# End of mixer 0 in a hybrid streaming encoder step: copies on ScalarE, paired products and splits, scales one step from the root

## The chip, the core and the metric

The kernel runs on one core of a Trainium2 chip. The metric is device time in microseconds of one launch. Three runs of the kernel before gave 1126.33, 1127.34 and 1127.87 us (median 1127.34). The engines are named as in the profile: PE (TensorE matmul), PEld (its weight loads), DVE (VectorE), ACT (ScalarE), POOL (GpSimd) and SP (the queue that issues the weight transfers). Each works through its own instructions in order; between engines there are only semaphores.

## The reference

One step of a two-layer encoder for 256 frames of a new stream and 8 running streams of 16 frames: 384 columns in all. Layer 0 has two mixers from one input projection:

```python
xa, ga, qb, kb, vb, gb, zr = jnp.split(u @ w_in, cuts, axis=-1)
ha, new_h = rg_lru(xa, lru_h0, ...)          # linear recurrence over time
ya = ha * jax.nn.gelu(ga)
o, new_S = gla(heads(qb) * DK_B ** -0.5, heads(kb), heads(vb), heads(log_g), gla_S0)
o = rms_norm(o, g_norm)                      # per head, over its 256 columns
yb = o * jax.nn.silu(gb)
y = jnp.concatenate([ya, yb], axis=-1) @ w_out
```

Then come an RMS norm with residual, a SwiGLU block, and layer 1 (latent attention and another SwiGLU). The change lies where `ya` and `o` are finished and `y` begins.

## The kernel before

**Numbers in two halves.** Every float32 product is made of three matmuls of rounded operands: high with high, high with low, low with high (L287, L288, L289 in `mm3`). An operand `x` is split by a Copy on ACT into its high part and a subtraction on DVE into its low part (`split`, L315 and L316).

**Weights.** `Stream` brings blocks of eight 128x128 tiles. SP transfers a block into one of three raw buffers (L98), ACT copies the high half (`whi`, L110), DVE subtracts for the low half (`wlo`, L126). When PE begins block n, the split of block n + 2 is issued: its `whi` at once, its `wlo` once half of block n's tiles have been taken. A raw buffer is free for its next transfer after the `wlo`. One projection of eight tiles is one block, 24 matmuls; `proj` issues it and then calls `tick`.

**Side work.** `tick` takes each generator in the list `sides` one step further, to its next `yield`. Thus the recurrence (`lru`) and the matrix state (`states`) are issued a piece at a time between the projections of the main line. What is issued at one place enters the queues of its engines there, behind all that was issued earlier: that alone sets the order on each engine.

**The main line here.** After the projections `gb` come eight projections `ga` (here ga0 to ga7). `lru` ends with products, scans (L800) and its state `hl` during ga0 and ga1. Behind ga1 `drain` runs `tick` until `lru` is done. Each `ga` is multiplied by its row factor on DVE (L978) into a tile that the trace calls `sq`; after each second one the pair is finished: Gelu on ACT (L996), product with `hl` on DVE (L998), split into `yah` and `yal` (L315, L316). Then the output projection `out_ab` starts, four output tiles at a time, over 16 input tiles: eight `yah`/`yal`, then eight `ybh`/`ybl`. `yb` is called one input tile ahead; its first seven calls are a `tick` each, the first of them loading the ACT table for Ln and Exp and marking "gelu" as done.

**`states`.** The new stream is worked in two chunks j = 0 and 1 of 128 frames; j = 2 stands for the running streams. For each j, `intra` (L826), and for chunk 1 also L915, put two heads' output each into a bank of PSUM; `grow_new` (L856) makes the state's growth, which ACT copies to `S1` (L906; tile `S` in the trace). `take(j, hp, bank)` copies a bank to `on[j]` (L829) and squares each head on ACT with a running sum (L831). Chunk 0 is issued in the `drain` behind ga1, chunk 1's matmuls behind ga3, its `take` behind ga4. `on[0]` and `on[1]` use slots 13 and 14, where input states S0 lay that L883 reads. In the first `tick` of `out_ab`, Ln and Exp (L929, L930) turn the sums into factors; `scale(j)` multiplies `on[j]` head by head on DVE (L835); `otrans(j)` transposes it on PE (L842) and ACT copies the result to `oT` (L843), from which L1075 to L1078 make `ybh` and `ybl`.

Of the kernel before, what the change touches and what calls it, by code (L numbers as in the profile page):

```python
# [10 lines left out]
AF = mybir.ActivationFunctionType  # L11
# [165 lines left out]
def emit(ctx, tc, A, O):  # L177
    nc = tc.nc
    v_, s_, g_, pe = nc.vector, nc.scalar, nc.gpsimd, nc.tensor
# [13 lines left out]
    def slot(k, shape, dt=F32, name="sl"):  # L193
        return sp.tile(shape, dt, name=nm(name), tag=f"s{k}", bufs=1)
# [6 lines left out]
    def mm_hold():  # L201
        return pr_.tile("mm", 6, [P, 512], hold=True)

    def sd(shape=(P, T)):
        return pr_.tile("sd", 2, shape)
# [4 lines left out]
    def sqt():  # L210
        return tr.tile("sq", 2, [P, T])

    def acct():
        return tr.tile("acc", 1, [P, T])
# [4 lines left out]
    def small(shape, name, bufs=4):  # L219
        return tr.tile(name, bufs, shape)  # L220

    def f(ap):
        return ap.bitcast(F32)
# [51 lines left out]
    def tick():  # L275
        for g in list(sides):
            try:
                next(g)
            except StopIteration:
                sides.remove(g)  # L280

    def drain(g):
        while g in sides:
            tick()
# [29 lines left out]
    def split(hi, lo, src):  # L314
        s_.activation(hi, src, AF.Copy)  # L315
        v_.tensor_sub(lo, src, f(hi))  # L316
# [37 lines left out]
    def proj(mat, mt, xk=None, kts=KD, side=True):  # L354
        xk = xk or uk
        ps = mm()
        for kt in range(kts):
            mm3(ps, S.take(mat, kt, mt), xk(kt), kt == 0, kt == kts - 1)
        if side:
            tick()  # L360
        return ps
# [23 lines left out]
    def quads(tiles):  # L385
        return lambda i: tiles[i // 4][:, i % 4, :]
# [425 lines left out]
    def states():  # L812
        while "chunks" not in done:
            yield
        kdT, qe = late["kdT"], late["qe"]
        sqs = small([P, 3, H_B], "osq", 1)
        on = {}

        def vh(j, h):
            return vt[h // 2][:, j, (h % 2) * 256:(h % 2) * 256 + 256]  # L820

        def half(bank, h):
            return bank[:, (h % 2) * 256:(h % 2) * 256 + 256]

        def intra(j, bank, h, stop):
            pe.matmul(half(bank, h), at[:, j, h, :], vh(j, h), start=True, stop=stop)  # L826

        def take(j, hp, bank):
            v_.tensor_copy(on[j][:, 2 * hp:2 * hp + 2, :], bank.rearrange("p (h v) -> p h v", h=2))  # L829
            for h in (2 * hp, 2 * hp + 1):  # L830
                s_.activation(acct()[:, 0:256], half(bank, h), AF.Square, accum_out=sqs[:, j, h:h + 1])  # L831

        def scale(j):
            for h in range(H_B):
                v_.tensor_scalar(on[j][:, h, :], on[j][:, h, :], sqs[:, j, h:h + 1], None, op0=OP.mult)  # L835

        def otrans(j):
            for hf in range(2):
                ps = sd([P, 4, P])
                for i in range(4):  # L840
                    fb = hf * 4 + i
                    pe.transpose(ps[:, i, :], on[j][:, fb // 2, (fb % 2) * P:(fb % 2) * P + P], ident)  # L842
                s_.activation(oT[hf][:, :, j * P:(j + 1) * P], ps, AF.Copy)  # L843

        def grow(product):

            res = []
            for hp in range(2):
                ps = sd([P, 2, 256])
                for k in (2 * hp, 2 * hp + 1):  # L850
                    product(ps[:, k % 2, :], k)
                res.append(ps)
            return res

        def grow_new(j):
            return grow(lambda ps, k: pe.matmul(ps, kdT[:, j, k, :], vh(j, k), start=True, stop=True))  # L856


        s0t = {}

        def s0load(i):
            s0t[i] = slot((13, 14, 3)[i % 3], [P, 4, 256], name="S0")
            g_.dma_start(s0t[i], A["S0"][i])

        s0load(0)
        s0load(1)
        on[2] = slot(6, [P, H_B, 256], name="on")
        for _ in range(2):
            yield
        while vt[1] is None:  # L870
            yield
        s0load(2)
        for i in range(2 * H_B):
            h, b0 = i // 2, 4 * (i % 2)
            if i % 4 == 0:
                bank, free = mm_hold()
            if b0 == 0:
                intra(2, bank, h, False)
            st = s0t.pop(i)
            for k in range(4):  # L880
                b = b0 + k
                o0 = 32 * (b // 2)
                pe.matmul(half(bank, h)[o0:o0 + 32], qe[:, 1 + b % 2, h, o0:o0 + 32], st[:, k, :],  # L883
                          start=False, stop=(b % 2 == 1))
            if i + 3 < 2 * H_B:
                s0load(i + 3)
            yield
            if i % 4 == 3:
                take(2, h // 2, bank)
                free()  # L890
        done.add("sample")

        while hl[1] is None:
            yield
        oT[0] = slot(16, [P, 4, T], name="oT")
        oT[1] = slot(4, [P, 4, T], name="oT")
        S1 = slot(0, [P, H_B, 256], name="S1")
        on[0] = slot(13, [P, H_B, 256], name="on")
        on[1] = slot(14, [P, H_B, 256], name="on")
        banks = [mm_hold() for _ in range(2)]  # L900
        for h in range(H_B):
            intra(0, banks[h // 2][0], h, True)
        gs = grow_new(0)
        yield
        for hp in range(2):
            s_.activation(S1[:, 2 * hp:2 * hp + 2, :], gs[hp], AF.Copy)  # L906
        for hp in range(2):
            take(0, hp, banks[hp][0])
            banks[hp][1]()
        yield  # L910
        yield
        banks = [mm_hold() for _ in range(2)]
        for h in range(H_B):
            intra(1, banks[h // 2][0], h, False)
            pe.matmul(half(banks[h // 2][0], h), qe[:, 0, h, :], S1[:, h, :], start=False, stop=True)  # L915
        yield
        gs = grow_new(1)
        for hp in range(2):
            take(1, hp, banks[hp][0])
            banks[hp][1]()  # L920
        yield
        for h in range(H_B):
            v_.scalar_tensor_tensor(S1[:, h, :], S1[:, h, :], ebl[:, h, 1:2], gs[h // 2][:, h % 2, :],
                                    op0=OP.mult, op1=OP.add)
        yield
        g_.dma_start(O["pS"], S1)
        while "gelu" not in done:
            yield
        s_.activation(sqs, sqs, AF.Ln, scale=1.0 / 256, bias=epsc)  # L929
        s_.activation(sqs, sqs, AF.Exp, scale=-0.5)  # L930
        yield
        for j in range(5):
            yield
            if j < 3:
                scale(j)
            if j >= 2:
                otrans(j - 2)

    side_lru, side_states = lru(), states()
    sides += [side_states, side_lru]  # L940
    for hf in range(2):
# [33 lines left out]
    for i in range(8):  # L975
        ps = proj("ga", i)
        z = sqt()
        v_.tensor_mul(z, ps, r0)  # L978
        if i % 2 == 0:
            z0 = z  # L980
            if i == 0:
                assert "sqrt" in done
                for t in sg:
                    s_.activation(t, t, AF.Silu)
            continue
        if i == 1:
            drain(side_lru)
            yah = [slot(k, [P, 4, T], F32R, name="yah") for k in (10, 15)]
            yal = [slot(5, [P, 4, T], F32R, name="yal")]
            yah_at, yal_at, hl_at = quads(yah), quads(yal), quads(hl)  # L990
        if i == 5:
            while "sample" not in done:
                tick()
            yal.append(slot(3, [P, 4, T], F32R, name="yal"))
        for z in (z0, z):
            s_.activation(z, z, AF.Gelu_apprx_tanh)  # L996
        for k, z in ((i - 1, z0), (i, z)):
            v_.tensor_mul(z, z, hl_at(k))  # L998
            split(yah_at(k), yal_at(k), z)


    carry = slot(12, [P, 3, 512], name="carry")
# [647 lines left out]
    for hq in range(2):  # L1650
        ps = mm(512)
        for i in range(8):
            h = 8 * hq + i
# [172 lines left out]
```

## Time and profile before

| what | value |
|---|---|
| median of three runs | 1127.34 us (1126.33 to 1127.87) |
| profiled execution, its own time | 1128.62 us |
| its span, first to last instruction | 1126.8 us |
| PE busy | 1098.3 us, 97% |
| DVE busy | 667.4 us, 59% |
| ACT busy | 541.5 us, 48% |
| POOL busy | 160.5 us, 14% |
| mean granted TensorE clock | 0.992 of full |

Busy time is that in which an engine has an instruction at work. Matmuls are pipelined, so a row's duration is longer than the step from one to the next. A granted clock of 1.00 is 2.4 GHz, 0.50 is 1.2 GHz; a value between is a mean over both. All times in rows are microseconds from the span's start.

### The profile page before, as it was taken

Reading aid. Unit: us, or ns where it says so; the run is one execution under the profiler, and the core shown is the slowest. Engines: PE = TensorE matmul, PEld = TensorE weight load, DVE = VectorE, ACT = ScalarE, POOL = GpSimd, SP = SyncE. Lnnn points to the kernel's source line nnn. Section 1 sums busy time; section 2 is a strip of 40 time slices with the busy share of each in tenths; the row PEclk is TensorE's granted clock in tenths of the full one; section 3 lists DMA queues with packets and bytes.
Section 4 is the critical chain, followed back from the end, with each engine's and each line's share of the span. In section 5 each row is a group of like instructions: output and inputs, shape, how many; then the busy total and the mean of one; then the engine's idle time right before and its main releaser. Section 6 shows DMA issues by size and latency. Waiting matters only on the chain. (4 is left out here: it accounts for less than half of the span.)

```text
span 1126.8 us, 16586 instructions
## 1 busy us (share of the span) xinstructions
PE 1098.3 (97%) x6463; PEld 1044.1 (93%) x6463; DVE 667.4 (59%) x1062; ACT 541.5 (48%) x927; POOL 160.5 (14%) x230
## 2 busy tenths in 40 slices
PE   9999999799999999999999999899999999999997
PEld 8989989699999999999999988699899999999886
DVE  5898774766276765554333777789347545554333
ACT  5642567554456333334334566677545443333232
POOL 3225110000230100000011211256122000000000
PEclk9999999899999999999999999999999999999999
DMA  8332552135434763334343351334324333443442
GB/s 265 100 95 93 187 169 88 65 127 178 128 95 156 255 224 127 117 130 130 117 129 101 113 168 61 121 126 147 113 94 132 131 122 122 131 127 119 128 131 75
DMA packets 43375, 147.50 MB, mean 131 GB/s; under 512 B 4928, under 2 KB 7616, under 8 KB 43296
## 3 DMA queue, kind: packets, MB, share of 16 engines
q1 hardware_dynamic: 39504, 132.73, 36.8%
q0 software_dynamic: 3792, 13.70, 3.6%
q8 instruction: 51, 0.84, 0.3%
q14 instruction: 28, 0.23, 0.1%
HBM read 139.53 MB, written 6.88 MB: 130 GB/s over the span
## 5 line engine op out<-in xcount | busy, mean ns | idle before, releaser
L126 DVE TENSOR_TENSOR wlo<-wraw,whi 128x1024 fp32r<-128x1024 f32 (+1 forms) x232 | 279.7, 1206 | 268.0 <-ACT whi L110 267.6
L287 PE MATMUL mm<-uhi,whi 128*128 128x384 f32 x1016 | 349.9, 344 | 9.6 <-ACT whi L110 6.2
L289 PE MATMUL mm<-ulo,whi 128*128 128x384 f32 x1016 | 344.8, 339 | 0.8 <-DVE ulo L312 0.8
L288 PE MATMUL mm<-uhi,wlo 128*128 128x384 f32 x1016 | 343.9, 338 | 0.9 <-DVE wlo L126 0.9
L110 ACT ACTIVATE whi<-wraw 128x1024 fp32r<-128x1024 f32 (+1 forms) x232 | 244.1, 1054 | 201.5 <-PE mm L289 134.5
L287 PEld LDWEIGHTS mm<-uhi,whi 128*128 128x128 f32 x1016 | 192.9, 190 | 13.7 <-ACT whi L110 6.6
L289 PEld LDWEIGHTS mm<-ulo,whi 128*128 128x128 f32 x1016 | 192.2, 189 | 2.2 <-DVE ulo L312 2.2
L288 PEld LDWEIGHTS mm<-uhi,wlo 128*128 128x128 f32 x1016 | 192.0, 189 | 1.8 <-DVE wlo L126 1.5
L337 POOL TENSOR_TENSOR acc<-acc,sq 128x384 f32<-128x384 f32 x43 | 53.0, 1232 | 346.6 <-ACT sq L336 346.1
L315 ACT ACTIVATE ah<-tmp 128x384 fp32r<-128x384 f32 x44 | 23.1, 525 | 80.0 <-DVE tmp L1183 80.0
L287 PE MATMUL mm<-ah,whi 128*128 128x384 f32 x176 | 59.8, 340 | 0.0
L1179 ACT ACTIVATE tmp<-tmp 128x384 f32<-128x384 f32 x44 | 22.9, 524 | 75.9 <-DVE tmp L1178 75.8
L289 PE MATMUL mm<-al,whi 128*128 128x384 f32 x176 | 59.1, 336 | 0.0
L288 PE MATMUL mm<-ah,wlo 128*128 128x384 f32 x176 | 59.1, 336 | 0.0
L1180 DVE TENSOR_TENSOR tmp<-mm,r 128x384 f32<-128x384 f32 x44 | 24.4, 556 | 44.4 <-PE mm L289 44.4
L297 PE MATMUL mm<-whi,ah 128*128 128x512 f32 x120 | 47.2, 393 | 0.0
L299 PE MATMUL mm<-whi,al 128*128 128x512 f32 x120 | 46.9, 391 | 0.0
L298 PE MATMUL mm<-wlo,ah 128*128 128x512 f32 x120 | 46.6, 388 | 0.0
L121 POOL TENSOR_TENSOR wlo<-wraw,whi 128x512 fp32r<-128x512 f32 x22 | 32.0, 1455 | 68.6 <-ACT whi L110 51.0
L316 DVE TENSOR_TENSOR al<-tmp,ah 128x384 fp32r<-128x384 f32 x44 | 24.6, 558 | 26.0 <-ACT ah L315 26.0
L287 PEld LDWEIGHTS mm<-ah,whi 128*128 128x128 f32 x176 | 33.1, 188 | 0.0
L288 PEld LDWEIGHTS mm<-ah,wlo 128*128 128x128 f32 x176 | 33.0, 188 | 0.0
(376 smaller groups left out, 1901.5 us busy)
## 6 DMA issues: line engine op xcount, KB each, us to landing
wraw<-wst SPq DMA_DIRECT2D x214, 512.0 KB, 3.6
S<-S POOLq DMA_DIRECT2D x16, 512.0 KB, 5.1
wraw<-cT SPq DMA_DIRECT2D x8, 528.0 KB, 3.7
o_sS<-S POOLq DMA_DIRECT2D x8, 512.0 KB, 4.2
wraw<-cN SPq DMA_DIRECT2D x8, 512.0 KB, 3.6
h<-x SPq DMA_DIRECT2D x2, 768.0 KB, 5.9
wuk<-wukT SPq DMA_DIRECT2D x2, 768.0 KB, 6.5
o_y<-hrow SPq DMA_DIRECT2D x6, 256.0 KB, 2.0
```

The source lines that it names most:

```text
L110: self.nc.scalar.activation(hi[:, s], raw[:, s], AF.Copy)
L121: self.nc.gpsimd.tensor_sub(*(x[:, n:] for x in a))
L126: self.nc.vector.tensor_sub(*a)
L287: pe.matmul(out, wl[0], xr[0], start=start, stop=False)
L288: pe.matmul(out, wl[1], xr[0], start=False, stop=False)
L289: pe.matmul(out, wl[0], xr[1], start=False, stop=stop)
L297: pe.matmul(ps[:, cs], xs[0][:, js], wh, start=start and i == 0, stop=False)
L298: pe.matmul(ps[:, cs], xs[0][:, js], wl, start=False, stop=False)
L299: pe.matmul(ps[:, cs], xs[1][:, js], wh, start=False, stop=stop and i + n == 4)
L316: v_.tensor_sub(lo, src, f(hi))
L337: g_.tensor_add(self.acc, self.acc, q)
L1180: v_.tensor_mul(w, pu, r)
```

## The change

Three edits. `take` copies `on[0]` and `on[1]` with ACT instead of DVE; the running streams' `on[2]` stays on DVE. At each second `ga` the two columns are finished step by step together (two products, two Copies, two subtractions) instead of one column after the other. After Ln and Exp one `yield` is gone and the loop has six steps instead of five: `scale(0)`, `scale(1)`, `scale(2)` are each issued one `tick` earlier, the three `otrans` in the same `tick` as before.

```diff
         def take(j, hp, bank):
-            v_.tensor_copy(on[j][:, 2 * hp:2 * hp + 2, :], bank.rearrange("p (h v) -> p h v", h=2))
+            on_hp, src = on[j][:, 2 * hp:2 * hp + 2, :], bank.rearrange("p (h v) -> p h v", h=2)
+            if j < 2:
+                s_.activation(on_hp, src, AF.Copy)
+            else:
+                v_.tensor_copy(on_hp, src)
             for h in (2 * hp, 2 * hp + 1):
                 s_.activation(acct()[:, 0:256], half(bank, h), AF.Square, accum_out=sqs[:, j, h:h + 1])
...
         s_.activation(sqs, sqs, AF.Ln, scale=1.0 / 256, bias=epsc)
         s_.activation(sqs, sqs, AF.Exp, scale=-0.5)
-        yield
-        for j in range(5):
+        for j in range(6):
             yield
             if j < 3:
                 scale(j)
-            if j >= 2:
-                otrans(j - 2)
+            else:
+                otrans(j - 3)
...
         for z in (z0, z):
             s_.activation(z, z, AF.Gelu_apprx_tanh)
-        for k, z in ((i - 1, z0), (i, z)):
+        pair = (i - 1, z0), (i, z)
+        for k, z in pair:
             v_.tensor_mul(z, z, hl_at(k))
-            split(yah_at(k), yal_at(k), z)
+        for k, z in pair:
+            s_.activation(yah_at(k), z, AF.Copy)
+        for k, z in pair:
+            v_.tensor_sub(yal_at(k), z, f(yah_at(k)))
```

## Rows read from the trace of the kernel before

**Rows 1.** Waits of PE, whole span: waiter <- releaser: us in total, times, longest.
```profile
PE mm L287 <- ACT whi L110: 6.2, 1, 6.2
...
PE sd L842 <- DVE on L835: 1.3, 1, 1.3
```
**Rows 2.** Timeline of PE: start, busy us, line, out<-in, count, [idle before <- releaser].
```profile
214.78 0.59 PE L915 MATMUL mm<-S,qe 128*128 128x256 f32 x2
221.53 0.69 PE L287 MATMUL mm<-uhi,whi 128*128 128x384 f32 x1 [6.16 <-ACT whi L110]
222.79 0.69 PE L288 MATMUL mm<-uhi,wlo 128*128 128x384 f32 x1 [0.57 <-DVE wlo L126]
...
229.49 1.89 PE L856 MATMUL sd<-v,kdT 128*128 128x256 f32 x8
...
231.39 0.34 PE L288 MATMUL mm<-uhi,wlo 128*128 128x384 f32 x1
...
235.25 0.34 PE L289 MATMUL mm<-ulo,whi 128*128 128x384 f32 x1
...
243.85 0.34 PE L287 MATMUL mm<-yah,whi 128*128 128x384 f32 x1
```
**Rows 3.** Windows, the wait: busy us (instructions) by engine, granted clock, DMA share, GB/s.
```profile
218.00:220.00 2.00, 0.00 (x0) 0.00 (x0) 1.39 (x3) 0.71 (x2) 0.00 (x0) 0.56 0.00 0
```
**Rows 4.** Timeline of ACT, from the state's copies to `whi` of ga4.
```profile
203.80 1.06 ACT L906 ACTIVATE S<-sd 128x512 f32<-128x512 f32 x2
213.96 0.38 ACT L831 ACTIVATE acc<-mm 128x256 f32<-128x256 f32 x1 [9.09 <-DVE on L829]
...
215.96 1.28 ACT L996 ACT_TABLE_LOAD   x1
217.25 0.94 ACT L996 ACTIVATE sq<-sq 128x384 f32<-128x384 f32 x2
...
220.01 0.52 ACT L315 ACTIVATE yah<-sq 128x384 fp32r<-128x384 f32 x1 [1.09 <-DVE sq L998]
220.44 1.99 ACT L110 ACTIVATE whi<-wraw 128x1024 fp32r<-128x1024 f32 x2
```
**Rows 5.** Timeline of DVE, from column 1's L978 to `wlo` of ga4.
```profile
212.79 0.53 DVE L978 TENSOR_TENSOR sq<-mm,r 128x384 f32<-128x384 f32 x1
213.24 1.28 DVE L829 COPY on<-mm 128x512 f32<-128x512 f32 x2
...
219.43 0.55 DVE L998 TENSOR_TENSOR sq<-sq,hl 128x384 f32<-128x384 f32 x1
...
221.51 1.22 DVE L126 TENSOR_TENSOR wlo<-wraw,whi 128x1024 fp32r<-128x1024 f32 x1 [0.39 <-ACT whi L110]
```
**Rows 6.** Readers of S0 (L883): ns min/median/max, first and last start us, form.
```profile
L883 PE MATMUL mm<-S,qe x64: 379/379/403, 134.1 to 182.3; 128*32 128x256 f32 x64
```
**Rows 7.** Windows: behind the wait for `on`, and around 730 us.
```profile
252.00:253.00 1.00, 1.00 (x9) 0.88 (x9) 1.00 (x5) 0.60 (x2) 0.00 (x0) 1.00 0.61 152
...
730.00:735.00 5.00, 2.42 (x14) 2.26 (x15) 2.88 (x9) 2.90 (x8) 1.27 (x5) 0.87 0.48 149
735.00:740.00 5.00, 5.00 (x35) 5.00 (x35) 4.30 (x13) 3.33 (x11) 2.97 (x2) 0.79 0.31 93
```
**Rows 8.** Timeline of PE around the first two transpose groups.
```profile
250.00 0.34 PE L289 MATMUL mm<-yal,whi 128*128 128x384 f32 x1
...
252.64 0.42 PE L287 MATMUL mm<-yah,whi 128*128 128x384 f32 x1
...
254.64 0.34 PE L289 MATMUL mm<-yal,whi 128*128 128x384 f32 x1
255.61 0.42 PE L287 MATMUL mm<-yah,whi 128*128 128x384 f32 x1
```
**Rows 9.** Timelines of ACT and DVE: the root's Exp, and eight scalings of `on`.
```profile
248.91 0.21 ACT L930 ACTIVATE osq<-osq 128x12 f32<-128x12 f32 x1
...
251.25 2.18 DVE L835 TENSOR_SCALAR on<-on,osq 128x256 f32<-128x256 f32 x8
```

## The prediction

> **What bounds the kernel now.** The page's first part comes first: PE is busy 97% of the span, DVE 59%, ACT 48%, so only time in which PE waits, or runs at its lower clock, can be won. Next the waits of PE, longest first [rows 1]: the longest of the whole span, 6.2 us, is a matmul waiting for a `whi` tile (the high half of a weight block, written on ACT); one of 1.3 us waits for DVE's scaling of `on`. Both lie in the part that the change edits.
>
> The timeline of PE shows the first one [rows 2]. PE ends the matmuls of stream chunk 1 (L915, two of them, 214.78 + 0.59 = 215.37), and projection ga4 starts only at 221.53. Its second matmul waits again, for `wlo`, until 222.79. The granted clock makes it dearer [rows 3]: its mean of 0.56 over 218 to 220 says that it fell from 2.4 to 1.2 GHz about 218.2, after 2.9 us without a matmul. From its second matmul to the L856 group behind it, ga4 took 229.49 - 222.79 = 6.70 us. The next projection ran at full clock: 22 steps from 231.39 to 235.25, 0.1755 us each, so that the same piece costs 23 x 0.1755 = 4.04 us. The clock thus cost 2.66 us on top of the wait.
>
> Why was `whi` late? ACT and DVE work in the order in which they were issued, and ACT had nothing to do from 204.86 to 213.96 [rows 4]: it stood at the first Square (L831), whose releaser is DVE's copy L829. DVE reached that copy at 213.24, behind both recurrent scans and product L978 [rows 5]. Then came, one after the other, four Squares (213.96 to 215.96, 0.50 each), a table load (1.28), two Gelus (0.94), and for each of two columns a product on DVE, a Copy `yah` on ACT and a subtraction on DVE. The second `yah` started at 220.01, and the `whi` of ga4 behind it at 220.44, of which PE's 221.53 is the answer.
>
> **The change, part by part.** *Copies on ACT, new streams' two chunks.* In the stretch of the wait two DVE copies (1.28 us) go, and ACT gets two copies of 128x512 out of PSUM. The nearest row is L906, the same shape from PSUM on ACT, two in 1.06 [rows 4]. Copy and Squares of one bank are then on one engine, so the wait for L829 is gone. Those copies follow L906 in the queue: 204.86 + 1.06 + 4 x 0.50 = 207.9, and the table load ends about 209.2. All of it lies in what was idle time of ACT; its cover is 9.1 us for 3.1 us of work. Were a copy to cost nothing or twice as much, the end would not move. The condition is that tiles `on[0]` and `on[1]` are free at 204.9. They take the place of old S0 tiles, whose last reader L883 started at 182.3 [rows 6]; so I take no wait.
>
> *What is then late.* Product L978 of column 1: it sits behind the scans, which the change does not touch, and ends 212.79 + 0.53 = 213.32 [rows 5]. With 0.04 us from engine to engine (it is 0.06 from `wlo`'s end, 221.51 + 1.22, to PE's 222.79), the chain is: second Gelu 213.36 to 213.88 (0.52, as the Copy's row); second product 213.92 to 214.47 (0.55); second `yah` 214.50 to 215.02. The first column's product and Copy fit ahead of each. *Products and Copies in pairs* matter here: DVE's first subtraction no longer stands ahead of the second product. `whi` of ga4 follows the second `yah` by 0.43, as before, at 214.93; `wlo` (L126) follows 1.07 later and takes 1.22 us, to 217.22 [rows 4, 5]. Against 220.01, `yah` starts 5.51 us earlier, and so do `whi`, `wlo` and PE. PE's first matmul of ga4 then starts at 216.02 and its second at 217.28; without any wait that would be 215.55. So some 1.7 us of the wait stay.
>
> *The clock.* PE would have two gaps, 0.65 us and, around one matmul, most of 1.2 us, in 215.37 to 217.28. The nearest stretch that kept 2.4 GHz is the 1.3 us wait of rows 1, right behind which the clock was 1.00 [rows 7]. The nearest that lost it lies at 730 to 735 [rows 7]: PE busy 2.42 of 5 us, clock 0.87, then 0.79 in the next five although PE was busy throughout. Mine, 1.9 us long, lies between and nearer the first; I take that the clock stays, which gives the 2.66 us back. The other end is a fall of the size of rows 7: (0.13 + 0.21) x 5 = 1.7 us lost.
>
> The Trainium skill's page "TensorE: Matmul & The Clock Gate" (section "A second HAM failure mode: psum-queue depth-cycling") says that short idles between groups of matmuls, frequent enough, also make the clock swing. Rows 7 agree, and by that rule the two gaps that are left would cost the lower clock again; it speaks against my choice and is rival A.
>
> *Until the output projection.* L856 behind ga4 then starts at 217.28 + 4.04 = 221.32, not 229.49: 8.17 us earlier = 5.51 + 2.66. ACT and DVE must follow at this pace. Counted on from 217 by the same durations, the `wlo` of ga5, ga6 and ga7 end at 218.9, 223.3 and 227.2, with the second chunk's copies (3.1 us of ACT) between the last two `whi`; PE wants them at 222.9, 227.1 and 231.3. All are early by 3.8 us or more. So the first output matmul (`yah`), 243.85 before, starts at 235.7: the shift is kept.
>
> *Pairs and scales before the transposes.* The second wait, at `otrans(0)`, shows as the time from the last matmul ahead to the first behind it: 252.64 - 250.00 = 2.64; the next transpose group, which waits for nothing, takes 255.61 - 254.64 = 0.97 [rows 8]. So 1.67 us are to be had. Before, the Exp of the root ended at 249.12 [rows 9], but `scale(0)` began only at 251.25, since a `wlo` stood ahead of it, which waited for a `whi` behind the root on ACT. After, `scale(0)` is issued one step earlier, ahead of that `wlo`: 249.16 + 1.1 (four operations, half of the 2.18 for eight) = 250.3. The pairing shortens the way to the root by about 0.9 us (the last product no longer waits for a subtraction, nor the Copy behind it), relative to PE. So `scale(0)` is done some 249.4 on the old scale, 0.8 us ahead of PE's arrival at 250.18. The `wlo` it passes starts at most 0.1 us later than its `whi` allows, and PE wants that block only after two more groups. `scale(1)` and `scale(2)` each have a group of 2.1 us more. Without the shortening `scale(0)` would be 0.1 us late, so at least 1.5 of the 1.67 stand on the step alone.
>
> *Sum.* 5.51 + 2.66 + 1.67 = 9.84 us. Nothing behind is tied to absolute time: the weights' transfers follow the freeing of their buffers, and PE is 97% busy. The profiled execution took 1128.62 us (span 1126.8), so it would take 1118.8; the median shown, 1127.34, lies 1.28 below the profiled one, and from it the forecast is 1127.34 - 9.84 = 1117.5.
>
> **The rivals.** A: the gaps that are left cost the clock, by 1.7 us: 1119.2. For it rows 7, against it that a 1.3 us wait, the larger part of what I expect, left the clock full.
>
> B: the change does not do what it says: ACT's copies are held until DVE is through L978, by a dependence on the tiles `on` that DVE's own order hides now. Then two copies and four Squares run from 213.35 to 216.4, the table load to 217.6, Gelus, products and `yah` to 219.7, `whi` from 219.69 and not 220.44. It gains 0.75, the clock still falls, and with 1.67 that is 2.4: 1124.9. For it: no row shows that the tiles are free before 213.24. Against it rows 6.
>
> C, slower: the clock falls in the gap and stays at 1.2 GHz while ga4 to ga7 run. A block of 24 matmuls costs 4.04 us more at half the clock, so from 9.84 / 4.04 = 2.4 slowed blocks the gain is gone, and with four it is 1117.5 + 16.2 = 1133.7. For it: before, the clock stayed low while PE was at work on most of ga4 [rows 2, 3]. Against it: by ga5 it was full again [rows 2].
>
> **How the numbers follow.** Forecast 0.60; A 0.27; B 0.06; C 0.02; the rest, 0.05, for a part of the second wait that stays (at most 1.67: 1119.2) or a wait of PE in ga5 to ga7. The forecast's own range is 1116 to 1118.5: the three runs spread over 1.5 us, and were the rest of the first wait also to go, it would be 1115.8. With A, and A together with the second wait left (1120.9), the range is 1115.7 to 1121.2, which leaves B and C out. A difference of 0.2%, 2.3 us, is about what a measurement of this kernel can tell from none; A, the forecast and B at its value lie beyond it, so faster 0.95, the same 0.03 (B, a little worse), slower 0.02.
>
> **What would show it.** Right: Square L831 for chunk 0 follows L906 with no idle time and the Gelu table load starts near 208; PE's wait for `whi` at ga4 is 0.7 us, not 6.2, with a second one under 1 us for `wlo`; the granted clock is 1.00 all through 216 to 230; L856 of chunk 1 starts near 221.3 and the first `yah` matmul near 235.7; PE waits for `on` no more; and from there to the end every row is earlier by the same 9.8 us. Wrong: a clock of 0.5 behind 217 (A, C), a first Square still at 213 or later (B), a new wait of PE for `whi` or `wlo` in ga5 to ga7, or a gain that is there at 260 and smaller at the end.

## The result, and the profile after

The changed kernel took 1117.87 us, the median of four runs (1116.89 to 1120.76), against 1127.55 us for the kernel before (four runs): 9.7 us less, a ratio of 0.9918 with a 95% interval of 0.9904 to 0.9932. The forecast was 1117.5, with a range of 1115.7 to 1121.2. A later measurement beside other kernels gave 1119.83 (five runs) against 1126.47, a ratio of 0.9941 (0.9928 to 0.9955), so 6.6 us; how the single runs scatter is told below, with the experiments.

In the changed kernel the line numbers move: L831 is the copy of `take` on ACT, L835 its Square, L981 the product with the row factor, L999 the Gelu, L1002 the product with `hl`, L1004 and L1006 the two halves `yah` and `yal`, L860 `grow_new`, L839 the scaling, L846 the transposes. The waits of PE over the whole span (waiter <- releaser: us in total, times, longest) no longer begin with those of [rows 1]:

```profile
PE mm L288 <- DVE wlo L126: 1.4, 3, 0.8
...
PE mm L287 <- ACT whi L110: 0.7, 1, 0.7
```

The wait for `whi` is 0.7 us and not 6.2, and there is none for `on`. The queue of ACT answers to [rows 4]:

```profile
201.29 1.06 ACT L910 ACTIVATE S<-sd 128x512 f32<-128x512 f32 x2
202.25 0.59 ACT L831 ACTIVATE on<-mm 128x512 f32<-128x512 f32 x1
...
205.09 1.28 ACT L999 ACT_TABLE_LOAD   x1
206.38 0.53 ACT L999 ACTIVATE sq<-sq 128x384 f32<-128x384 f32 x1
210.87 0.52 ACT L999 ACTIVATE sq<-sq 128x384 f32<-128x384 f32 x1 [3.96 <-DVE sq L981]
...
212.01 0.52 ACT L1004 ACTIVATE yah<-sq 128x384 fp32r<-128x384 f32 x1 [0.16 <-DVE sq L1002]
212.44 1.99 ACT L110 ACTIVATE whi<-wraw 128x1024 fp32r<-128x1024 f32 x2
```

Everything in this execution came 2.5 us sooner than in the one before already at the state's copies (201.29 against 203.80), in a part where nothing changed; that has to be taken off first. Two things account for it that the execution of before has and this one has not: a wait of 0.8 us of PE for DVE (L595), and a fall of the granted clock long ahead of the change, about 1.7 us, since 0.17 of full speed is missing over ten us. The windows of before, then after, show the fall (the columns are those of [rows 3]).

```profile
10.00:20.00 10.00, 8.35 (x37) 7.52 (x36) 8.04 (x7) 7.35 (x13) 4.53 (x4) 0.83 1.01 346
10.00:20.00 10.00, 8.54 (x46) 7.72 (x46) 8.26 (x7) 7.12 (x13) 4.54 (x4) 1.00 1.02 351
```

The copies start where the state's copies end, with no idle time, and the table load is over at 206.37, hidden. ACT then waits 3.96 us for one thing, DVE's product of column 1 (L981), which the scans hold. From the state's copies to the second `yah` it is 10.72 us, before it was 16.21: 5.49 less. DVE shows the pair, two products in one row, and `wlo` of ga4, which answers to [rows 5]:

```profile
210.30 0.53 DVE L981 TENSOR_TENSOR sq<-mm,r 128x384 f32<-128x384 f32 x1
210.75 1.23 DVE L1002 TENSOR_TENSOR sq<-sq,hl 128x384 f32<-128x384 f32 x2
211.90 1.23 DVE L1006 TENSOR_TENSOR yal<-sq,yah 128x384 fp32r<-128x384 f32 x2
213.52 1.22 DVE L126 TENSOR_TENSOR wlo<-wraw,whi 128x1024 fp32r<-128x1024 f32 x1 [0.39 <-ACT whi L110]
```

PE, which answers to [rows 2, 8]:

```profile
212.29 0.59 PE L919 MATMUL mm<-S,qe 128*128 128x256 f32 x2
213.54 0.44 PE L287 MATMUL mm<-uhi,whi 128*128 128x384 f32 x1 [0.66 <-ACT whi L110]
214.79 0.44 PE L288 MATMUL mm<-uhi,wlo 128*128 128x384 f32 x1 [0.82 <-DVE wlo L126]
...
218.94 1.89 PE L860 MATMUL sd<-v,kdT 128*128 128x256 f32 x8
...
233.31 0.33 PE L287 MATMUL mm<-yah,whi 128*128 128x384 f32 x1
...
239.45 0.34 PE L289 MATMUL mm<-yal,whi 128*128 128x384 f32 x1
239.63 1.03 PE L846 MATMUL sd<-ident,on 128*128 128x128 f32 x8
240.42 0.42 PE L287 MATMUL mm<-yah,whi 128*128 128x384 f32 x1
```

From the last L919 to ga4's second matmul it is 2.50 us, before 8.01. From there to L860 it is 4.15 us, before 6.70: no block at the lower clock, 1.2 GHz. Around the first transposes it is 0.97 us, before 2.64. The granted clock in the windows of the remaining gap and of a later stretch:

```profile
210.00:214.00 4.00, 3.27 (x13) 2.01 (x12) 3.37 (x7) 2.98 (x5) 1.39 (x4) 1.00 0.10 37
214.00:216.00 2.00, 1.21 (x7) 1.21 (x8) 2.00 (x3) 0.96 (x2) 0.00 (x0) 1.00 0.26 37
216.00:218.00 2.00, 2.00 (x13) 2.00 (x12) 1.81 (x5) 0.94 (x2) 0.00 (x0) 1.00 0.82 254
720.00:725.00 5.00, 3.78 (x22) 3.81 (x23) 3.88 (x10) 3.43 (x9) 1.21 (x1) 0.72 0.29 106
725.00:730.00 5.00, 5.00 (x42) 5.00 (x41) 3.88 (x11) 2.73 (x9) 2.68 (x3) 0.94 0.42 144
```

The clock stayed at 2.4 GHz through the gap; the fall that the kernel before had at 730 to 740 [rows 7] is still there, at 720 to 730. So between the last L919 and the matmul behind the first transposes the change saved 37.86 - 28.13 = 9.73 us; the spans differ by 11.7, of which 2.5 lie ahead of it, and -0.5 behind. The 13 profiled executions, which all run the same code behind that matmul, take 874.2 to 876.2 us for it, so 0.5 us there can't be told from scatter.

### The profile page after: what moved, and what is told of

The parts are those of the page before. It is cut to its first block, busy times and chain, and to the rows that moved or that the text cites. A ratio compares the mean times of both kernels' runs of the same rounds, so it can differ in the third digit from the quotient of the medians.

```text
span 1115.1 us, 16588 instructions
## 1 busy us (share of the span) xinstructions
PE 1093.4 (98%) x6463; PEld 1039.6 (93%) x6463; DVE 666.1 (60%) x1058; ACT 543.1 (49%) x931; POOL 161.5 (14%) x230
## 5 line engine op out<-in xcount | busy, mean ns | idle before, releaser
L289 PEld LDWEIGHTS mm<-al,whi 128*128 128x128 f32 x176 | 33.0, 188 | 0.0
```

Of the source, the lines that this page charges most:

```text
L289: pe.matmul(out, wl[0], xr[1], start=False, stop=stop)
```

## The experiments

All were timed beside the kernel before, and the ratios are to its runs there: a median of 1127.46 (29 runs) for the copies, the pairs, the scales and the 11 ones; 1126.47 (9 runs) for the 22 ones with pairs and scales and for the second values of the changed kernel, without and with the early split; 1127.55 (4 runs) for the changed kernel's first value; 1127.48 (21 runs) for the others. A range in brackets behind a gain is its 95% interval. Three lengths of PE's timeline, in one profiled execution of each kernel, say most: A from the last matmul of chunk 1 to ga4's second matmul, B from there to the second `grow_new`, C around the first transposes (last matmul ahead to first behind), in us.

| kernel | median us (runs) | ratio to before, 95% interval | A | B | C |
|---|---|---|---|---|---|
| before | 1127.46 (29) | | 8.01 | 6.70 | 2.64 |
| changed | 1117.87 (4), 1119.83 (5) | 0.9918, 0.9941 | 2.50 | 4.15 | 0.97 |
| copies alone | 1122.98 (6) | 0.9953 (0.9936 to 0.9971) | 3.44 | 5.52 | 2.64 |
| pairs alone | 1125.28 (12) | 0.9976 (0.9966 to 0.9986) | 6.87 | 6.20 | 1.75 |
| scales alone | 1125.51 (12) | 0.9979 (0.9968 to 0.9989) | 8.02 | 5.58 | 0.97 |
| 11 matmuls of ones | 1127.70 (12) | 0.9997 (0.9987 to 1.0007) | 8.02 | 5.43 | 2.74 |
| 22 matmuls of ones | 1126.38 (11) | 0.9992 (0.9981 to 1.0003) | 8.03 | 4.14 | 3.97 |
| 22 ones, pairs, scales | 1122.73 (5) | 0.9968 (0.9955 to 0.9980) | 6.87 | 4.15 | 0.96 |
| ga4's split early, before | 1125.23 (11) | 0.9976 (0.9967 to 0.9985) | 0.93 | 4.14 | 2.47 |
| changed, copies thrice | 1117.96 (5) | 0.9916 (0.9902 to 0.9929) | 2.51 | 4.15 | 0.96 |
| changed, ga4's split early | 1115.77 (5), 1116.34 (4) | 0.9896, 0.9912 | 0.61 | 4.03 | 0.97 |

**Each part alone.** The copies:

```diff
-            v_.tensor_copy(on[j][:, 2 * hp:2 * hp + 2, :], bank.rearrange("p (h v) -> p h v", h=2))
+            on_hp, src = on[j][:, 2 * hp:2 * hp + 2, :], bank.rearrange("p (h v) -> p h v", h=2)
+            if j < 2:
+                s_.activation(on_hp, src, AF.Copy)
+            else:
+                v_.tensor_copy(on_hp, src)
```

> The kernel before with the copies of on[0] and on[1] moved to ACT, and nothing else of the change. Theory (the terms add up: ACT was held by DVE's copy): the second Gelu ends where it does in the changed kernel, but the first column's subtraction stands ahead of the second product on DVE, so the second yah starts 0.95 us later than in the changed kernel; the wait at ga4 shrinks by 4.56 instead of 5.51 us, PE idles 1.6 us and then 0.6 to 0.8 us, and the 1.3 us wait for on stays (a gap of 2.6 us around the first transposes). If the clock stays full the gain is 4.56 + 2.66 = 7.2 us (about 1120.3 us); if it falls for a short while, 5.5 (about 1122). Rival (the copies alone make the whole gain): about 1117.9.

Measured 4.5 us (3.3 to 7.2), below the 5.5 of the expectation with a fall of the clock, but within the noise of it; by the lengths it is 5.8. Length A shrank by 4.57 us, as worked out (4.56). The clock fell, though for less long than before: B is 5.52. PE's waits from 190 to 260 us, and the clock behind them:

```profile
PE mm L287 <- ACT whi L110: 1.6, 1, 1.6
PE sd L846 <- DVE on L839: 1.3, 1, 1.3
PE mm L288 <- DVE wlo L126: 0.8, 1, 0.8
```

```profile
215.00:220.00 5.00, 3.51 (x11) 3.26 (x12) 4.02 (x6) 3.03 (x5) 0.00 (x0) 0.66 0.36 111
```

Gaps of 1.6 and 0.8 us about one matmul cost the clock here; 0.66 and 0.82 did not in the three profiled executions with those gaps (two of the changed kernel, one with its copies done three times). So the pairing may be worth more than its 0.94 us of A, by keeping the clock up. That is not shown: of the copies alone one execution was profiled, and elsewhere like gaps cost the clock in one execution and not in another (last section). The copies are not the whole gain.

The pairs (the third part of the diff of the change, on the kernel before):

> The kernel before with the paired products, Copies and subtractions alone. Theory: ACT still stands at the Square until DVE's copy; the second yah starts 1.15 us earlier, PE still idles some 5 us and the clock still falls; the root comes 0.9 us earlier, so the gap at the first transposes shrinks from 2.64 to about 1.7 us. Gain 1.15 + 0.9 = about 2 us (1125.5). Rival (the pairing is what makes the weight block early): a gain of 5 us or more and no fall of the clock.

2.2 us, with A 1.14 and C 0.89 shorter, as expected to 0.02 us. The first wait stays (waits from 190 to 260 us):

```profile
PE mm L287 <- ACT whi L110: 5.0, 1, 5.0
PE mm L288 <- DVE wlo L126: 0.6, 1, 0.6
PE sd L842 <- DVE on L835: 0.4, 1, 0.4
```

The scales (the second part alone):

> The kernel before with the scales one step earlier alone. Theory: the first scale starts right behind the root's Exp, the gap at the first transposes falls from 2.64 us to about 1.1, the wait of 6.2 us and the low clock at ga4 stay: gain 1.5 us (1126.0). Rival (the transposes only wait for the root, so the step needs the pairing to bring anything): gain under 0.5 us.

2.0 us; C fell to 0.97, the whole of 1.67, without any pairing. DVE shows why: four scalings start as soon as Exp is done (L930 is the releaser), and the `wlo` comes behind them.

```profile
247.39 1.14 DVE L835 TENSOR_SCALAR on<-on,osq 128x256 f32<-128x256 f32 x4 [1.30 <-ACT osq L930]
248.44 1.22 DVE L126 TENSOR_TENSOR wlo<-wraw,whi 128x1024 fp32r<-128x1024 f32 x1
249.58 2.19 DVE L835 TENSOR_SCALAR on<-on,osq 128x256 f32<-128x256 f32 x8
```

**The clock by itself.**

```diff
...
         ps = mm()
+        for _ in range(idle):
+            pe.matmul(ps[:, 0:P], ones, ones, start=True, stop=True)
...
-        ps = proj("ga", i)
+        ps = proj("ga", i, idle=11 if i == 4 else 0)
```

> The kernel before with eleven matmuls of ones ahead of ga4 (about 5 us of PE work that the sum does not need, into the bank that ga4 then overwrites); ACT and DVE are as before. Theory: whi still comes at 221.5 on the old scale, but the clock does not fall, so ga4 takes 4.04 instead of 6.70 us and the kernel gains 2.66 us (about 1124.9). Rival (the clock's price is hidden, because ga5 would wait for its weights anyway): gain 0.5 us or less.

No gain. Eleven were too few: they took 2.62 us, PE then idled 3.71, and the clock fell all the same (B 5.43). So it says little of the clock's price, and a second run was made.

> The kernel before with 22 instead of 11 matmuls of ones ahead of ga4: in the run with eleven they took 2.62 us, so these take some 5.2 and PE idles about 0.9 us, not 3.7, before whi comes. Theory: the clock stays at 2.4 GHz, ga4 takes 4.04 us from its second matmul to the next group, and the gain is what the clock costs: 2.66 us in the profiled execution of the kernel before, 1.5 and 2.2 in those of the runs with scales and pairs alone, so 1125 to 1126. Rival (the clock's price is no real time, as the run with eleven seemed to say): within 0.7 us of the kernel before.

The clock held: B is 4.14, 2.56 us shorter. But the kernel gained 1.1 us by the medians, with an interval that includes none. The timeline of PE in this kernel, and its wait for `on`, show where it went (each of the 22 is two instructions in the trace):

```profile
215.40 5.07 PE L358 MATMUL mm<-ones 128*128 128x128 f32 x44
221.74 0.44 PE L287 MATMUL mm<-uhi,whi 128*128 128x384 f32 x1 [1.26 <-ACT whi L110]
223.00 0.44 PE L288 MATMUL mm<-uhi,wlo 128*128 128x384 f32 x1 [0.82 <-DVE wlo L126]
...
227.14 1.89 PE L858 MATMUL sd<-v,kdT 128*128 128x256 f32 x8
```

```profile
PE sd L844 <- DVE on L837: 2.6, 1, 2.6
```

C grew from 2.64 to 3.97: 1.33 of the 2.56 us were given back at the transposes, because DVE, which has to scale `on` first, was not as much earlier as PE: counted from the state's copies, its first scaling starts after 46.31 us, before after 47.45, so 1.14 us earlier. So the terms do not add on the kernel before. They should add where the scales and pairs are in place too, with the copies still on DVE:

> The kernel before with the pairs and the scales of the change, without its copies, and with the 22 matmuls of ones that held the clock. Theory (the three terms add once none of them is given back at the transposes): the first wait shrinks by 1.15 us only, the clock's 2.6 us are kept, since the earlier root and the earlier scale take up what the run with ones alone gave back, and of the gap at the transposes 1.4 to 1.67 go: 5.2 us (about 1122.3). Rival (without the copies on ACT the clock's part is always given back later): 3.3 us or less (1124.2), with a gap of over 2 us at the first transposes.

1122.73 us against 1126.47 beside it: 3.7 us less (2.3 to 5.1), nearer the rival's 3.3 than the 5.2 that was expected. The lengths speak for the theory: A is 1.14 shorter, B 4.15, C 0.96, so 1.14 + 2.55 + 1.68 = 5.4 us, nothing of it given back at the transposes, where the rival wanted a gap of over 2 us. Behind them this execution took 2.0 us longer than that of before, with a granted clock of 0.71 over 785 to 790 us where that of before had 1.00. So the terms add as far as the transposes; that all of it reaches the end is not shown.

**Is it only the block's place in the queue?**

```diff
         if i == 1:
+            S.split()
             drain(side_lru)
+            S.flush()
```

> The kernel before with the split of ga4's block issued ahead of the drain (whi) and its subtraction behind the drain (wlo), and nothing of the change. Theory (PE waited only because the block stood behind the pair on ACT; the copies on ACT are one way to move it): the wait at ga4 falls to 0.2 us, and ga5's block, still behind the pair, is late by about 1.4 us; the clock mostly stays; gain 5.5 to 8 us (1119.5 to 1122), with the gap at the first transposes unchanged at 2.6 us. Rival (DVE's copies must leave DVE for any gain): under 2 us.

This theory of mine fell: 2.25 us (1.7 to 3.7), not 5.5 to 8, and so near the rival's bound of 2 that the number does not speak against the rival. A is 0.93, so PE hardly waits at ga4. But then it waits again and again, as these rows of its timeline show:

```profile
213.76 0.45 PE L288 MATMUL mm<-uhi,wlo 128*128 128x384 f32 x1 [0.16 <-DVE wlo L126]
220.87 0.44 PE L288 MATMUL mm<-uhi,wlo 128*128 128x384 f32 x1 [0.82 <-DVE wlo L126]
226.20 0.44 PE L288 MATMUL mm<-uhi,wlo 128*128 128x384 f32 x1 [0.82 <-DVE wlo L126]
231.04 0.45 PE L288 MATMUL mm<-uhi,wlo 128*128 128x384 f32 x1 [0.36 <-DVE wlo L126]
236.66 0.45 PE L287 MATMUL mm<-yah,whi 128*128 128x384 f32 x1 [1.31 <-ACT whi L110]
237.92 0.69 PE L288 MATMUL mm<-yah,wlo 128*128 128x384 f32 x1 [0.81 <-DVE wlo L126]
```

From the second `grow_new` to the first `yah` matmul it took 18.76 us, in every other kernel of the table 14.4. The clock fell too: 0.79 over 235 to 240 us and 0.87 over the next five. With DVE's copies ahead of the Squares and the columns one at a time, ACT and DVE finish the first pair hardly sooner (its second `yah` starts 15.3 us behind the state's copies, 16.2 before), and each later block stands behind it. Moving one block only moves the wait; the copies and the pairing shorten the chain itself.

**Copies three times, on the changed kernel.**

```diff
-                s_.activation(on_hp, src, AF.Copy)
+                for _ in range(3):
+                    s_.activation(on_hp, src, AF.Copy)
```

> The changed kernel with each of the four copies on ACT done three times (eight more copies of 0.5 us, four per chunk). Theory (all of it lies in ACT's idle time): the second Gelu of the first pair starts at the same time behind DVE's product, the whi of ga7 comes 2.1 us later and is still early, and the time is that of the changed kernel, 1117.9 within 0.7. Rival (ACT's queue is on the path): 2 to 4 us slower than the changed kernel.

1117.96 us: the same. The copies on ACT cost nothing that can be measured, and neither do 2.5 us more of them per chunk; behind those of chunk 0 ACT still stands idle for 1.41 us, waiting for DVE's product of column 1.

**What is left of the wait.**

```diff
         if i == 1:
             drain(side_lru)
+            S.split()
+            S.flush()
```

The first text is of this edit; the second and third are of the changed kernel and of this edit once more, measured side by side.

> The changed kernel with the split of ga4's weight block issued right behind the drain, ahead of the pair of Gelus, products and Copies (whi on ACT in its idle time, wlo on DVE ahead of the two products). Theory (what is left of the wait is only the place of this block in the queues): PE does not wait at ga4, 1.7 us more are gained (about 1116.1), ga5's block is ready 3 us before PE wants it. Rival (the chain of the recurrence itself limits PE, so the wait moves to ga5 or to the output projection): within 0.7 us of the changed kernel (1117.9).

> The changed kernel as it is, beside the next one on the same chip. Both theories: 1117.9 within 0.7.

> The changed kernel with ga4's split issued right behind the drain, once more, beside the changed kernel. Theory (the rest of the wait, 1.7 us, and with it any fall of the clock there, is gone for good): 1.7 to 2.3 us faster than the changed kernel. Rival (the 2.1 us between their medians are the spread of few runs): within 0.7 us of it.

On the changed kernel the early split works. First 1115.77 us; then, side by side, 1116.34 against 1119.83, with ratios to before of 0.9912 (0.9898 to 0.9925) and 0.9941 (0.9928 to 0.9955) that just do not touch: 3.5 us there, 2.1 by the first medians, 1.9 by length A (0.61 against 2.50) and 0.1 by B. So some 2 us are accounted for, as expected; the 3.5 lie above the 1.7 to 2.3 that were expected of the second measurement. PE shows no wait at ga4:

```profile
215.05 0.59 PE L919 MATMUL mm<-S,qe 128*128 128x256 f32 x2
215.29 0.53 PE L287 MATMUL mm<-uhi,whi 128*128 128x384 f32 x1
```

This version beats both kernels in both measurements. Its two profiled executions show a fall of the clock at 780 to 790 us that the two of the changed kernel do not have, and side by side their spans differ by 1.0 us only (1114.2 against 1115.2); whether that fall belongs to this version is open.

The 1119.83 lies above the 1117.9 that was expected of the changed kernel. Over both measurements its nine runs fall into five from 1116.89 to 1118.10 and four from 1119.83 to 1120.89; the mean granted clock is 0.995 to 0.998 in the five and 0.994 to 0.996 in the four. Both profiled ones are among the five, so none of the four can be looked into. The two profiled executions of the early split differ as much, 1118.88 and 1115.97 us, and there the place is seen: already at the last L919 the first is 3.11 us behind (215.05 against 211.94), and its clock fell at 10 to 20 us:

```profile
10.00:20.00 10.00, 7.84 (x34) 7.01 (x33) 7.69 (x7) 7.02 (x12) 4.52 (x4) 0.83 0.99 333
10.00:20.00 10.00, 8.65 (x47) 7.82 (x46) 8.55 (x7) 7.18 (x14) 4.55 (x4) 1.00 1.01 350
```

In five of the 13 profiled executions the clock fell there, with a mean of 0.83 each time, and the last matmul of chunk 1 starts at 214.1 to 215.1 us; in the other eight it stayed at 1.00, and that matmul starts at 211.7 to 213.5. No edit touches this part. So such a fall, rather than one in the gap at ga4, is the likelier reason for the four longer runs; it is not shown for them.

## Why the prediction was right

*First wait, 5.51 us.* Measured 5.49 to 5.51. The reading held that ACT was idle at a Square, and that its releaser was a DVE copy standing behind the scans. Why a Square should wait for a copy that only reads the same bank, no run here shows by itself. The Trainium skill's page "PSUM — Partial Sum Buffer" (section "PSUM bank collisions raise a hardware error") gives a reason: two engines that touch one bank in the same partitions at once, reads with reads included, raise an error, and the compiler's scheduler adds a dependency between such instructions. The trace agrees with such an order: 9.09 us of wait in [rows 4], none in the changed kernel, where copy and Square are both on ACT. Not tested is the plainer rival that needs no move at all, the Squares issued ahead of DVE's copies, which might free ACT as well. `on[0]` was free, so rival B is out.

*The clock, 2.66 us.* B shrank by 2.55 in the profile (4.15, not the 4.04 worked out); the clock was full, so rivals A and C did not happen in the profiled executions. C's price was too high besides: at a granted clock of 0.50 the matmuls of ga4 in the kernel before start 0.32 us apart (15 steps from 223.28 to 228.08), not twice 0.1755, so a slowed block costs 24 x 0.1445 = 3.5 us more and not 4.04. But the term was weaker than it looked in two ways. The 6.70 us of the one profile of before is at the dear end: with the same wait, B was 5.58 where only the scales were moved. And the 22 ones showed that half of it is given back at the transposes if nothing is done there. The prediction called the shift "kept" as far as the first `yah` and treated the second wait as a term of its own; it did not say that the one needs the other. The sum held because the change does both. The rule of rival A, for which the prediction cites the Trainium skill's page "TensorE: Matmul & The Clock Gate" (section "A second HAM failure mode: psum-queue depth-cycling"), is that frequent short idles between groups of matmuls also make the clock swing. The traces agree in kind: gaps of 1.6 and 0.8 us (copies alone) were followed by the lower clock; but 1.26 and 0.82 (22 ones) and 0.66 and 0.82 (changed) were not. That the clock would stay was a choice between two rows, at 0.60 against 0.27, and not something that the rows gave.

*Second wait, 1.67 us.* Measured 1.67. Alone, the step brought all of it and not only 1.5.

*The rest.* Blocks ga5 to ga7 were early as worked out: the distance from the second `grow_new` to the first `yah` is 14.37 us, before 14.36. The sum, 9.84, was 9.73 in the profile as far as the transposes, 9.2 from the state's copies to the end, and 9.7 by the first medians, 6.6 by the later ones. The mechanism was right term by term; that the first median lies within 0.4 us of the forecast is in part luck, since single runs of the changed kernel spread over 4 us and the clock's term was read from one execution at the dear end.

## What to carry to other kernels

When a wait of the bounding engine names a releaser, follow that engine's own queue back to where it stood idle: here a Square on ACT waited for a copy on DVE, which waited behind a scan, and PE paid for it ten us later. Then ask of every gain where the next engine will be: a stall removed on PE alone (by holding the clock, or by moving one block) came back at the next place where ACT or DVE was late. Work that the idle engine can do costs nothing as long as the idle time lasts, and a short gap can be dear by the clock behind it, in one execution and not in the next. Before comparing two profiles, compare them ahead of the change: here 2.5 us of difference lay there.

## What was not expected of the hardware

The same stall does not cost the same each time. With the same wait of 6.2 us, ga4 took 6.70 us in one execution and 5.58 in another (the scales alone, whose code is the same here), against 4.15 at full clock; and 29 runs of the kernel before spread from 1125.04 to 1131.05 us. Of a change of 1 us one profile on each side says little; lengths between rows of the same execution say more. PE in the run with the scales alone, to be set beside [rows 2]:

```profile
220.87 0.69 PE L287 MATMUL mm<-uhi,whi 128*128 128x384 f32 x1 [6.16 <-ACT whi L110]
222.13 0.69 PE L288 MATMUL mm<-uhi,wlo 128*128 128x384 f32 x1 [0.57 <-DVE wlo L126]
...
227.71 1.89 PE L856 MATMUL sd<-v,kdT 128*128 128x256 f32 x8
```

Small gaps behave in the same way. At 11 to 14 us PE waits up to three times in a row, in a part that no edit touches. These are the first and the third of these waits in the kernel before, and then in the run with the copies alone:

```profile
11.62 0.45 PE L287 MATMUL mm<-uhi,whi 128*128 128x384 f32 x1 [0.50 <-ACT uhi L311]
...
13.66 0.69 PE L289 MATMUL mm<-ulo,whi 128*128 128x384 f32 x1 [0.83 <-DVE ulo L312]
```

```profile
11.42 0.44 PE L287 MATMUL mm<-uhi,whi 128*128 128x384 f32 x1 [0.78 <-ACT uhi L311]
...
13.45 0.44 PE L289 MATMUL mm<-ulo,whi 128*128 128x384 f32 x1 [0.83 <-DVE ulo L312]
```

The wait between them is 0.31 us in both. With the shorter waits the clock fell (a mean of 0.84 over 10 to 15 us), with the longer ones it stayed at 1.00. So the length of the gaps alone did not decide here whether the clock fell.
